# Tap pairs over all 128 rows in a key compression, and rotation tables of the index heads ahead of the others

## The chip, the core and the metric

The kernel runs on one core of one Trainium2 chip. The metric is device time in microseconds of one execution. In the profile, PE is TensorE's matmul, PEld its weight load, DVE is VectorE, ACT is ScalarE, POOL is GpSimd and SP is SyncE, which here issues nearly all DMAs.

## The reference, cut to what matters

Two decoder layers over 256 tokens of width 1024, float32. Each has a token mixer, a cross-attention into 256 memory tokens and a SwiGLU FFN. Layer 0's mixer holds a sparse attention whose index heads score every key (rotated index queries against rotated index keys, ReLU, a weighted sum over 8 heads), keep the top 64 keys of each query, and attend to them. Layer 1's mixer has among its branches a compressed one:

```
def nsa_compress(x, pos_emb, w1, w2):              # x (1, 256, 4 groups, 64)
    n_cmp = (S - 32) // 16 + 1                     # 15 blocks of 32 tokens, 16 apart
    blk = x[:, idx] + pos_emb[None, None, :, None, :]
    blk = ....reshape(B, n_cmp, G, 32 * 64)
    return jax.nn.silu(blk @ w1) @ w2              # w1 (2048, 64), w2 (64, 64)
```

It runs once for keys and once for values, with weights of their own. Rotation (`partial_rope`) multiplies pairs of elements by cosines and sines of position times frequency. The index heads use it without a gain; the other heads use it with their norm's gain, which the kernel folds into their tables.

## The kernel before, in words

**Order of the work.** The program is unrolled by Python coroutines. A planner (`Steps`, `Est`) keeps an estimated clock for each engine and issues, again and again, the operation that can start first; among those within 0.03 us on one engine the lower rank goes first, then the earlier, then the one spawned first. Every engine then runs its list strictly in that order. One helper (line 252) puts out all compute instructions, so nearly every row bears that line, and rows are told apart by their tiles. An instruction whose operand is late holds up all that stand behind it on its engine. An operation with two ways (`move`, `tt`) goes to the engine that the planner thinks sooner. For a DMA the planner only notes an assumed landing time.

**Weights.** A coroutine `pusher` (line 458 on) takes 256 rows by 512 columns of a weight matrix at a time from a `raw` tile (3 of them), makes a rounded part `hi` (ACT or DVE) and a remainder `lo` (DVE, one `TENSOR_TENSOR` into `whl`), and issues the load of the pair three further on, on SP's queue. Six `whl` pairs can stand ready. Every large product is three float32r matmuls (`mm3`) into PSUM banks that the profile calls `mm` and, in the FFN's second product, also `po`.

**The start.** `tables()` (line 550), rank 3, makes angles from positions on DVE, sine and cosine on ACT, then waits until the first norm has written both halves of row tile 0 (`has(("mix0", 0), 2)`), and then makes the gain rows, the index heads' tables `ia` and `ib`, the other heads' tables `ra` and `rb`, and the masks `cm`, `cmn`, `cmi`; at its end it sets the flag `tables`. `ev_small` takes the first product's result (index queries, index keys and one key head) out of PSUM, waits for `tables`, rotates the index queries (`rope`), transposes, and so releases `index()`, whose sums on DVE are followed by `top()`: eight rounds of finding and striking out eight maxima, on DVE. The attention over the chosen keys waits for that (`bias`). The other three products of this mixer go on meanwhile.

**The compression.** `load_cmp()` is started when layer 0's FFN has issued its first products. It loads `w1` into four tiles, 64 rows of keys' weights above 64 rows of values' weights, `w2`, and the position rows. At the mixer's start `prep()` transposes the position rows into a fifth group of the tile `kvT`, and `ev_kc` writes there, row tile by row tile, the transposed keys (rows 0 to 63) and values (rows 64 to 127). `compress()` then goes over the 32 taps. Each tap has two matmuls, one for keys, one for values, each over 64 rows into 64 output rows, with 75 moving columns (5 groups of 15 blocks, 16 elements apart):

```
yield T.matmul(hps[64 * i:64 * i + 64, :NB], w1[tt // 8][0][64 * i:64 * i + 64, tt % 8, :],
         kvT[64 * i:64 * i + 64, :, tt:tt + 16 * (NCMP - 1) + 1:16],
         start=(tt == 0), stop=(tt == 31), tile_position=(64 * i, 64 * i))
```

The fifth group's column is the share of the position rows, copied to `pb` and used as the bias of the SiLU. After every 8 taps the coroutine lets at least one `mm3` of another product go in between. A float32 matmul stands in the trace as two pairs of a weight load and a matmul, so 64 matmuls are 128 records of each kind.

Of the kernel before, what the change touches and what calls it, by code (L numbers as in the profile page):

```python
# [8 lines left out]
F32 = mybir.dt.float32  # L9
F32R = mybir.dt.float32r  # L10
# [5 lines left out]
P = 128  # L16
# [72 lines left out]
class Steps:  # L89
# [7 lines left out]
    def spawn(self, g, rank=2):  # L97
        self.n += 1
        self.new.append([rank, self.n, g, None])
# [253 lines left out]
def trunk(ctx: ExitStack, tc: tile.TileContext, I, out):  # L353
# [196 lines left out]
    def tables():  # L550
# [21 lines left out]
        yield from ready(AF.Exp)  # L572
        yield has(("mix0", 0), 2)
# [17 lines left out]
        gv = growt.rearrange("p j (a b) -> p j a b", a=2)  # L591
        for h in range(2):
            yield V.tensor_copy(ia[:, :, h, :], cos[:, :, ::2])
            yield V.tensor_copy(ib[:, :, h, :], (sin if h else nsin)[:, :, ::2])
        for t in range(NT):
# [115 lines left out]
    def root(key, t):  # L711

        yield lambda: (key, t) in vr
        return vr[key, t]
# [124 lines left out]
    def mixer0():  # L839
# [11 lines left out]
        def ev_small(ps, free, t):  # L851
# [88 lines left out]
        def ev_q(j, key):  # L940
            def ev(ps, free, t):
                q, qf = yield from T2.get([P, 8, HD])
                yield move(q.rearrange("p h d -> p (h d)"), ps)
                yield from inv_rms(ps, 8, HD, (yield from root("mix0", t))[0], 1.0, HD, rq[j, t], free)
                yield from rope(q, 8, ra[:, t, 2 * j], rb[:, t, 2 * j], HALF)
# [12 lines left out]
        def ev_k(ps, free, t):  # L958
            q, qf = yield from T2.get([P, 8, HD])
            yield S.activation(q.rearrange("p h d -> p (h d)"), ps, AF.Copy)  # L960
            rk = tiny(8, "rk8")
            yield from inv_rms(ps, 8, HD, (yield from root("mix0", t))[0], 1.0 / HD, 1.0, rk, free)
            yield from rope(q, 8, ra[:, t, 3], rb[:, t, 3], HALF)
            dd, df = yield from T4.get([P, 8, 2, HD])
# [78 lines left out]

    def load_cmp():
        w2 = hp.tile([P, P], F32, name="w2")
        pos = hp.tile([32, P], F32, name="posemb")
        yield PO.memset(w2, 0.0)
        w1 = []
        for j in range(4):
            w = yield from SL.get([P, 8, HD])  # L1050
            w1.append(w)
            for i, s in enumerate("kv"):
                nc.sync.dma_start(w[0][64 * i:64 * i + 64],
                                    I[f"nsa_cmp_w1_{s}"][0, 512 * j:512 * j + 512].rearrange("(t d) h -> d t h", d=HD))
        for i, s in enumerate("kv"):
            nc.sync.dma_start(w2[64 * i:64 * i + 64, 64 * i:64 * i + 64], I[f"nsa_cmp_w2_{s}"][0])
            nc.sync.dma_start(pos[:, 64 * i:64 * i + 64], I[f"nsa_cmp_pos_{s}"][0])
        w1s.update(w1=w1, w2=w2, pos=pos)
        done("cmpw")

    def mixer1():
# [3 lines left out]
        gt = [hp.tile([P, G * HG, 3], F32, name=f"gt{t}") for t in range(NT)]  # L1065
        kvT = hp.tile([P, G + 1, SEQ], F32, name="kvT", tag="kvT")
# [4 lines left out]
        def prep():  # L1071
            yield has("cmpw")
            yield PO.memset(kvT[:, G, 32:], 0.0)
            ps, f = yield from TP.get([P, 512])
            yield T.transpose(ps[:, :32], w1s["pos"], ident[:32, :32])
            yield V.tensor_copy(kvT[:, G, :32], ps[:, :32])
            f()
            done("kvT")

        def ev_kc(ps, free, t):  # L1080
            c, cf = yield from T2.get([P, G, 2, HD])
            yield S.activation(c, ps.rearrange("p (b g d) -> p g b d", b=2, g=G), AF.Copy, scale=(yield from root("mix1", t))[1])
            free()
            tps, f = yield from TP.get([P, 512])
            for g in range(G):
                yield T.transpose(tps[:, g * P:(g + 1) * P], c[:, g].rearrange("p a d -> p (a d)"), ident)
            yield S.activation(kvT[:, :G, t * P:(t + 1) * P], tps.rearrange("p (a b) -> p a b", a=G), AF.Copy)
            f()
            cf()
            done("kvT")  # L1090

        def compress():
            yield has("kvT", 3)
            NB = (G + 1) * NCMP
            N = G * NCMP
            w1 = w1s["w1"]
            hps, hf = yield from PV.get([P, 512])
            for tt in range(32):
                if tt % TAPS == 0 and tt:
                    yield has("mm", flags["mm"] + 1)  # L1100
                for i in range(2):
                    yield T.matmul(hps[64 * i:64 * i + 64, :NB], w1[tt // 8][0][64 * i:64 * i + 64, tt % 8, :],
                             kvT[64 * i:64 * i + 64, :, tt:tt + 16 * (NCMP - 1) + 1:16],
                             start=(tt == 0), stop=(tt == 31), tile_position=(64 * i, 64 * i))
            for w in w1:
                w[1]()
            pb = tiny(1, "pb")
            yield V.tensor_copy(pb, hps[:, N:N + 1])
            hs = tp.tile([P, N], F32, name="hs")
            yield S.activation(hs, hps[:, :N], AF.Silu, bias=pb)  # L1110
            hf()
# [200 lines left out]
        h = [hsel(t) for t in range(NT)]  # L1312
        spawn(prep())
        spawn(compress())
# [48 lines left out]
    def mem_k(L):  # L1363
        kT = [hp.tile([P, MH, SEQ], F32R, name=f"mkT{e}") for e in range(2)]
        mkv[L, "k"] = kT
# [273 lines left out]
```

## Time and profile before

| | |
|---|---|
| three timed runs | 784.57, 785.92, 786.65 us (median 785.92) |
| the profiled execution | 785.81 us, of which the span is 784.0 |
| PE busy | 757.2 us (97%) |
| DVE, ACT, POOL busy | 531.3, 435.7, 122.7 us (68%, 56%, 16%) |
| mean granted TensorE clock | 0.995 |

The span runs from the first to the last instruction, and 1.8 us of the execution's time lie around it. A busy share is a mean over stages: the start, the two mixers and the FFNs differ. In the list of records a matmul's duration holds its way through the array too, and neighbours overlap, so the pace of a run of matmuls is read from the distance between starts.

### The profile page before, as it was taken

Reading aid. Unit: us, or ns where it says so; the run is one execution under the profiler, and the core shown is the slowest. Engines: PE = TensorE matmul, PEld = TensorE weight load, DVE = VectorE, ACT = ScalarE, POOL = GpSimd, SP = SyncE. Lnnn points to the kernel's source line nnn. Section 1 sums busy time; section 2 is a strip of 40 time slices with the busy share of each in tenths; the row PEclk is TensorE's granted clock in tenths of the full one; section 3 lists DMA queues with packets and bytes.
Section 4 is the critical chain, followed back from the end, with each engine's and each line's share of the span. In section 5 each row is a group of like instructions: output and inputs, shape, how many; then the busy total and the mean of one; then the engine's idle time right before and its main releaser. Section 6 shows DMA issues by size and latency. Waiting matters only on the chain.

```text
span 784.0 us, 11770 instructions
## 1 busy us (share of the span) xinstructions
PE 757.2 (97%) x4227; PEld 629.6 (80%) x4227; DVE 531.3 (68%) x1111; ACT 435.7 (56%) x819; POOL 122.7 (16%) x169
## 2 busy tenths in 40 slices
PE   6898899999999999999999999999999999999998
PEld 5777687798888888878788787887888888889886
DVE  6899998778655545555717889978767546546542
ACT  5677786566545444344525889846656444444440
POOL 1554430210000000000106365301200000000000
PEclk9999899999999999999999999999999999999999
DMA  6735424435465554777524723034435566546761
GB/s 213 207 101 162 147 96 159 164 108 168 156 210 179 164 185 122 203 243 229 172 58 129 219 77 110 14 122 163 160 115 167 162 201 188 165 130 214 221 184 54
DMA packets 70635, 122.32 MB, mean 156 GB/s; under 512 B 8549, under 2 KB 15793, under 8 KB 70577
## 3 DMA queue, kind: packets, MB, share of 16 engines
q1 hardware_dynamic: 70544, 121.58, 49.7%
q8 instruction: 33, 0.54, 0.3%
q14 instruction: 26, 0.20, 0.1%
q0 software_dynamic: 32, 0.00, 0.0%
HBM read 120.51 MB, written 1.05 MB: 155 GB/s over the span
## 4 chain that ended last, share of the span: by engine, by line
PE 73%; DVE 10%; DMA 6%; ACT 4%; POOL 3%; issue 3%; SPq 1%; ACTq 0%; POOLq 0%; DVEq 0%
PE mm L252 56%; PE po L252 9%; PE tp L252 6%; DVE whl L252 3%; DMA raw<-in_ffn_w_out 3%; PE sp L252 3%; DVE place L252 3%; ACT whl L252 2%; ACT place L252 2%; DMA raw<-in_nsa_w_in 2%; POOL rope L252 1%; DMA raw<-in_ab_w_in 1%; POOL place L252 1%; DVE hss L252 1%; DMA raw<-in_nsa_w_out 1%
## 5 line engine op out<-in xcount | busy, mean ns | idle before, releaser
L252 PE MATMUL mm<-whl,h 128*128 128x512 f32 (+3 forms) x1776 | 400.4, 379 | 3.6 <-DVE whl L252 3.2
L252 DVE TENSOR_TENSOR whl<-raw,whl 128x1024 fp32r<-128x1024 f32 (+3 forms) x232 | 272.2, 1180 | 135.6 <-ACT whl L252 133.4
L252 PEld LDWEIGHTS mm<-whl,h 128*128 128x128 f32 x1776 | 310.5, 189 | 60.8 <-DVE whl L252 4.1
L252 ACT ACTIVATE whl<-raw 128x1024 fp32r<-128x1024 f32 (+3 forms) x216 | 218.3, 1012 | 193.0 <-PE mm L252 75.4
L252 PE MATMUL mm<-whl,place 128*128 128x512 f32 (+1 forms) x840 | 195.3, 376 | 0.9 <-DVE x L252 0.8
L252 PEld LDWEIGHTS mm<-whl,place 128*128 128x128 f32 x840 | 143.4, 190 | 28.2 <-DVE x L252 1.6
L252 PE MATMUL po<-whl,place 128*128 128x512 f32 x264 | 68.1, 395 | 0.0
L252 ACT ACTIVATE place<-tp 128x512 f32<-128x512 f32 (+4 forms) x115 | 54.7, 500 | 20.9 <-PE tp L252 20.4
L252 PEld LDWEIGHTS po<-whl,place 128*128 128x128 f32 x264 | 49.4, 188 | 11.4
L252 PE MATMUL tp<-ident,place 128*128 128x128 f32 (+1 forms) x340 | 53.1, 276 | 4.7 <-POOL place L252 2.3
L252 PEld LDWEIGHTS tp<-ident,place 128*128 128x128 f32 (+1 forms) x340 | 40.1, 140 | 13.9 <-issue 3.5
L252 ACT ACTIVATE place<-place,mx 128x128 f32<-128x128 f32 (+1 forms) x96 | 42.9, 453 | 7.7 <-DVE mx L252 6.6
L252 POOL TENSOR_TENSOR place<-place,rc 128x512 f32<-128x512 f32 (+2 forms) x33 | 29.7, 900 | 41.2 <-DVE rc L252 29.0
L252 POOL TENSOR_TENSOR rh<-vh,mhalf 128x1 f32<-128x1 f32 x12 | 9.9, 826 | 148.5 <-DVE vh L252 132.2
L252 ACT ACTIVATE h<-place 128x512 fp32r<-128x512 f32 x23 | 14.4, 628 | 33.0 <-DVE place L252 33.0
L252 DVE TENSOR_TENSOR x<-mm,x 128x512 f32<-128x512 f32 x36 | 24.5, 684 | 10.3 <-PE mm L252 10.2
L252 DVE CUSTOM_DVE_ANT_0 place<-sp,cm,rq 128x128 f32<-128x128 f32 (+1 forms) x80 | 30.3, 407 | 1.3 <-PE sp L252 1.2
L252 ACT ACTIVATE place<-mm 128x512 f32<-128x512 f32 (+2 forms) x45 | 23.0, 553 | 14.3 <-PE mm L252 14.3
L252 ACT ACTIVATE place<-mm,rh 128x512 f32<-128x512 f32 (+1 forms) x26 | 17.0, 654 | 22.4 <-PE mm L252 22.4
L252 DVE SCALAR_TENSOR_TENSOR place<-mm,rh,place 128x512 f32<-128x512 f32 (+1 forms) x24 | 16.9, 704 | 18.1 <-PE mm L252 18.1
L252 POOL TENSOR_TENSOR h<-place,h 128x512 fp32r<-128x512 f32 x1 | 1.3, 1294 | 175.9 <-ACT h L252 175.9
L252 PE MATMUL sp<-place,place 128*128 128x256 f32 x160 | 27.1, 300 | 0.0
(202 smaller groups left out, 620.4 us busy)
## 6 DMA issues: line engine op xcount, KB each, us to landing
raw<-in_ffn_w_in SPq DMA_DIRECT2D x80, 512.0 KB, 4.3
raw<-in_ffn_w_out SPq DMA_DIRECT2D x44, 512.0 KB, 4.3
raw<-in_ab_w_in SPq DMA_DIRECT2D x16, 512.0 KB, 4.1
raw<-in_mem_w_kv SPq DMA_DIRECT2D x16, 512.0 KB, 3.9
raw<-in_nsa_w_in SPq DMA_DIRECT2D x16, 512.0 KB, 4.1
raw<-in_ab_w_out SPq DMA_DIRECT2D x8, 512.0 KB, 3.8
raw<-in_mem_w_q SPq DMA_DIRECT2D x8, 512.0 KB, 4.0
raw<-in_mem_w_o SPq DMA_DIRECT2D x8, 512.0 KB, 4.1
```

The costliest lines, as they stand in the source:

```text
L252: return f(*a, **{q: v() if q in ("start", "stop") and callable(v) else v for q, v in k.items()})
```

## The change

`tables()` gets rank 2; right after the cosine it makes `ia` and `ib`, sets a new flag `angles`, and leaves the rest to a new coroutine `gains()` of rank 3. `ev_small` waits for `angles` before it rotates the index heads, and for `tables` only before it rotates the key head; the other three rotations of this mixer get a wait for `tables`.

In the compression, taps `j` and `j + 16` form a pair. There are now two tiles `kvT[i]` in place of one, with the elements in the order tap, group, block. `ev_kc` writes keys into rows 0 to 63 of the first and values into rows 64 to 127 of the second, and when both row tiles are there, two DMAs on ACT's queue copy each to the other 64 rows, one element on, which is the next block of the same tap. A matmul then goes over 128 rows (both taps of the pair) into 64 output rows with 60 moving columns (4 groups, each of 15 neighbouring blocks); keys and values take the two column halves of the array. `load_cmp` loads `w1` in the matching order, the position rows with two DMAs more, and itself works out the position rows' share, `pb`, by products with `w1` and sums on DVE or POOL and a matmul of one column. `prep()` is gone. The new tiles take the tag of the memory keys `mkT`.

```
@@ tables
+        for h in range(2):
+            yield V.tensor_copy(ia[:, :, h, :], cos[:, :, ::2])
+            yield V.tensor_copy(ib[:, :, h, :], (sin if h else nsin)[:, :, ::2])
+        done("angles")
+        spawn(gains(sin, nsin, cos), 3)
+
+    def gains(sin, nsin, cos):
+        yield has(("mix0", 0), 2)
...
@@ ev_small
-            yield has("tables")
+            yield has("angles")
             yield from rope(c[:, 128:384].rearrange("p (h d) -> p h d", h=IH), IH, ia[:, t], ib[:, t], IHALF)
...
+            yield has("tables")
             yield from rope(k, 1, ra[:, t, 1], rb[:, t, 1], HALF)
...
@@ load_cmp
+        for i, s in enumerate("kv"):
+            for j in range(2):
+                w = yield from SL.get([P, 8, HD])
+                w1.append(w)
+                for b in range(2):
+                    d0 = HD * (16 * (b ^ i) + 8 * j)
+                    nc.sync.dma_start(w[0][64 * b:64 * b + 64], I[f"nsa_cmp_w1_{s}"][0, d0:d0 + 512].rearrange("(t d) h -> d t h", d=HD))
+                est.note(w[0], est.wr, clk["PE"] + 8.0, "D")
...
+        est.note(pos, est.wr, clk["PE"] + 8.0, "D")
+        ps, f = yield from TP.get([P, 512])
+        yield T.transpose(ps[:, :32], pos, ident[:32, :32])
+        yield V.tensor_copy(pT.rearrange("p a b -> p (a b)"), ps[:, :32])
+        f()
+        for i in range(2):
+            u = []
+            for j in range(2):
+                u.append((yield from SL.get([P, 8, HD])))
+                yield tt(u[j][0], w1[2 * i + j][0], pT[:, i, 8 * j:8 * j + 8, None].to_broadcast([P, 8, HD]), OP.mult)
+            yield tt(u[0][0], u[0][0], u[1][0], OP.add)
+            u[1][1]()
+            yield V.tensor_reduce(red[:, i], u[0][0].rearrange("p t h -> p h t"), axis=AX.X, op=OP.add)
+            u[0][1]()
+        ps, f = yield from TP.get([P, 512])
+        yield T.matmul(ps[:, :1], red.rearrange("p a b -> p (a b)"), one, start=True, stop=True)
+        yield V.tensor_copy(pb, ps[:, :1])
...
@@ ev_kc
-            yield S.activation(kvT[:, :G, t * P:(t + 1) * P], tps.rearrange("p (a b) -> p a b", a=G), AF.Copy)
+            for i in range(2):
+                r = slice(64 * i, 64 * i + 64)
+                yield S.activation(kvT[i][r, :, :, 8 * t:8 * t + 8].rearrange("p j g n -> p g n j"),
+                                   tps[r].rearrange("p (g n j) -> p g n j", g=G, n=8), AF.Copy)
...
+                for i in range(2):
+                    a, b = (kvT[i][64 * e:64 * e + 64].rearrange("p j g n -> p (j g n)") for e in (i, 1 - i))
+                    nc.scalar.dma_start(b[:, :-1], a[:, 1:])
+                    est.note(b, est.wr, clk["S"] + 3.0, "D")
...
@@ compress
-            for tt in range(32):
-                if tt % TAPS == 0 and tt:
+            for j in range(16):
+                if j % TAPS == 0 and j:
                     yield has("mm", flags["mm"] + 1)
...
+                yield together([T.matmul(hps[64 * i:64 * i + 64, :N], w1s["w1"][2 * i + j // 8][0][:, j % 8, :],
+                                         kvT[i][:, j, :, :NCMP], start=(j == 0), stop=(j == 15), tile_position=(0, 64 * i))
+                                for i in range(2)])
...
-    spawn(tables(), 3)
+    spawn(tables(), 2)
```

## Rows read from the trace of the kernel before

**Rows 1.** The page's first part: busy time and share of each engine.

```profile
PE 757.2 (97%) x4227; PEld 629.6 (80%) x4227; DVE 531.3 (68%) x1111; ACT 435.7 (56%) x819; POOL 122.7 (16%) x169
```

**Rows 2.** Stretches: us; busy PE, PEld, DVE, ACT, POOL; PEclk, DMA share, GB/s.

```profile
8.70:20.00 11.30, 10.62 (x43) 9.20 (x44) 11.09 (x27) 8.04 (x17) 1.08 (x2) 1.00 0.73 216
20.00:42.00 22.00, 18.98 (x85) 14.85 (x84) 17.89 (x60) 14.37 (x24) 12.33 (x22) 1.00 0.74 214
42.00:60.00 18.00, 17.80 (x104) 14.59 (x105) 16.85 (x40) 13.64 (x26) 9.89 (x18) 1.00 0.25 69
60.00:72.00 12.00, 11.02 (x55) 8.73 (x53) 12.00 (x33) 7.99 (x16) 5.88 (x8) 1.00 0.40 126
72.00:79.00 7.00, 5.66 (x30) 4.42 (x29) 7.00 (x29) 6.10 (x12) 1.82 (x1) 1.00 0.81 258
79.00:87.30 8.30, 7.24 (x47) 5.96 (x45) 8.27 (x46) 6.15 (x25) 3.36 (x5) 1.00 0.19 69
87.30:94.20 6.90, 5.13 (x30) 3.92 (x29) 6.87 (x16) 5.50 (x11) 3.41 (x3) 0.65 0.51 174
331.00:376.00 45.00, 43.99 (x189) 34.96 (x187) 22.66 (x19) 19.10 (x18) 0.00 (x0) 1.00 0.73 232
...
89.40:96.30 6.90, 6.43 (x25) 5.10 (x26) 6.82 (x20) 5.88 (x15) 2.20 (x2) 0.51 0.72 237
```

**Rows 3.** The chain of waits, 300 to 460 us: start, length, what.

```profile
324.37 1.39 PE po L252 x6
325.76 0.30 SPq L1053
...
400.31 2.18 PE po L252 x32
402.50 0.43 PE mm L252
...
409.11 2.19 PE po L252 x32
```

**Rows 4.** Instructions in order of time on PE, 495.9 to 500 us: start, length.

```profile
496.10 0.97 PE L252 MATMUL sp<-kbd,place 128*128 128x30 f32 x8
496.91 0.72 PE L252 MATMUL sp<-place,place 128*128 128x256 f32 x4
...
498.27 1.04 PE L252 MATMUL po<-place,place 120*64 120x128 f32 x16
499.24 0.98 PE L252 MATMUL sp<-place,place 128*128 128x256 f32 x6
```

**Rows 5.** Instructions in order of time, 0 to 42 us: the index heads' way.

```profile
18.75 0.51 ACT L252 ACTIVATE place<-mm 128x424 f32<-128x424 f32 x1
...
24.70 0.21 ACT L252 ACTIVATE cos<-ang 128x16 f32<-128x16 f32 x1
...
28.44 0.15 DVE L252 COPY ia<-cos 128x8 f32<-128x8 f32 x1
...
28.66 0.16 DVE L252 COPY ib<-sin 128x8 f32<-128x8 f32 x1
...
31.48 0.32 POOL L252 TENSOR_TENSOR rope<-place,ia 128x64 f32<-128x64 f32 x1
```

**Rows 6.** SP's issues in order of time, 310 to 335 us: first and last of twelve.

```profile
321.23 0.72 SPq L1053 DMA_DIRECT2D place<-in_nsa_cmp_w_k  x1
...
330.00 0.58 SPq L1057 DMA_DIRECT2D posemb<-in_nsa_cmp_pos_v  x1
```

**Rows 7.** Instructions in order of time, 346 to 394 us: end of layer 0's FFN.

```profile
374.17 1.23 DVE L252 TENSOR_TENSOR whl<-raw,whl 128x1024 fp32r<-128x1024 f32 x1 [1.26 <-ACT whl L252]
375.31 0.68 DVE L252 TENSOR_TENSOR x<-mm,x 128x512 f32<-128x512 f32 x1
376.05 0.66 PE L252 MATMUL tp<-ident,x 128*128 128x128 f32 x4 [0.93 <-DVE x L252]
```

**Rows 8.** DMA issues by group: count, KB each, us from issue to landing.

```profile
out_x<-x SPq DMA_DIRECT2D x4, 256.0 KB, 2.0
```

More of the change, by code (lines that the diff above doesn't have):

```diff
@@ L591, in tables @@
         gv = growt.rearrange("p j (a b) -> p j a b", a=2)
-        for h in range(2):
-            yield V.tensor_copy(ia[:, :, h, :], cos[:, :, ::2])
-            yield V.tensor_copy(ib[:, :, h, :], (sin if h else nsin)[:, :, ::2])
         for t in range(NT):
@@ L944, in ev @@
                 yield from inv_rms(ps, 8, HD, (yield from root("mix0", t))[0], 1.0, HD, rq[j, t], free)
+                yield has("tables")
                 yield from rope(q, 8, ra[:, t, 2 * j], rb[:, t, 2 * j], HALF)
@@ L962, in ev_k @@
             yield from inv_rms(ps, 8, HD, (yield from root("mix0", t))[0], 1.0 / HD, 1.0, rk, free)
+            yield has("tables")
             yield from rope(q, 8, ra[:, t, 3], rb[:, t, 3], HALF)
@@ L1046, in load_cmp @@
         pos = hp.tile([32, P], F32, name="posemb")
+        pT = hp.tile([P, 2, 16], F32, name="posT")
+        red = hp.tile([P, 2, HD], F32, name="posw")
+        pb = hp.tile([P, 1], F32, name="posb")
         yield PO.memset(w2, 0.0)
         w1 = []
[L1049 to L1054, printed above, removed]
+        for i, s in enumerate("kv"):
[6 more added lines that the diff above has]
+                est.note(w[0], est.wr, clk["PE"] + 8.0, "D")
@@ L1055, in load_cmp @@
         for i, s in enumerate("kv"):
             nc.sync.dma_start(w2[64 * i:64 * i + 64, 64 * i:64 * i + 64], I[f"nsa_cmp_w2_{s}"][0])
-            nc.sync.dma_start(pos[:, 64 * i:64 * i + 64], I[f"nsa_cmp_pos_{s}"][0])
-        w1s.update(w1=w1, w2=w2, pos=pos)
+            for b in range(2):
+                nc.sync.dma_start(pos[16 * i:16 * i + 16, 64 * b:64 * b + 64], I[f"nsa_cmp_pos_{s}"][0, 16 * (b ^ i):16 * (b ^ i) + 16])
+        est.note(pos, est.wr, clk["PE"] + 8.0, "D")
+        ps, f = yield from TP.get([P, 512])
@@ L1065, in mixer1 @@
         gt = [hp.tile([P, G * HG, 3], F32, name=f"gt{t}") for t in range(NT)]
-        kvT = hp.tile([P, G + 1, SEQ], F32, name="kvT", tag="kvT")
+        kvT = [hp.tile([P, 16, G, 16], F32, name=f"kvT{i}", tag=f"mkT{i}") for i in range(2)]
         kbd = hp.tile([P, G, 2, NCMP], F32, name="kbd")
@@ L1069, in mixer1 @@
         vbig = {}
[L1071 to L1078, printed above, removed]
         def ev_kc(ps, free, t):
@@ L1090, in ev_kc @@
             done("kvT")
+            if has("kvT", NT)():
+                for i in range(2):
+                    a, b = (kvT[i][64 * e:64 * e + 64].rearrange("p j g n -> p (j g n)") for e in (i, 1 - i))
+                    nc.scalar.dma_start(b[:, :-1], a[:, 1:])
+                    est.note(b, est.wr, clk["S"] + 3.0, "D")
+                done("kvT")
         def compress():
             yield has("kvT", 3)
-            NB = (G + 1) * NCMP
             N = G * NCMP
+            yield has("cmpw")
             w1 = w1s["w1"]
             hps, hf = yield from PV.get([P, 512])
-            for tt in range(32):
-                if tt % TAPS == 0 and tt:
+            for j in range(16):
+                if j % TAPS == 0 and j:
                     yield has("mm", flags["mm"] + 1)
[L1101 to L1104, printed above, removed]
+                yield together([T.matmul(hps[64 * i:64 * i + 64, :N], w1s["w1"][2 * i + j // 8][0][:, j % 8, :],
+                                         kvT[i][:, j, :, :NCMP], start=(j == 0), stop=(j == 15), tile_position=(0, 64 * i))
+                                for i in range(2)])
             for w in w1:
                 w[1]()
-            pb = tiny(1, "pb")
-            yield V.tensor_copy(pb, hps[:, N:N + 1])
             hs = tp.tile([P, N], F32, name="hs")
-            yield S.activation(hs, hps[:, :N], AF.Silu, bias=pb)
+            yield S.activation(hs, hps[:, :N], AF.Silu, bias=w1s["pb"])
             hf()
@@ L1312, in mixer1 @@
         h = [hsel(t) for t in range(NT)]
-        spawn(prep())
         spawn(compress())
@@ L1363, in mem_k @@
     def mem_k(L):
-        kT = [hp.tile([P, MH, SEQ], F32R, name=f"mkT{e}") for e in range(2)]
+        kT = [hp.tile([P, MH, SEQ], F32R, name=f"mkT{e}", tag=f"mkT{e}") for e in range(2)]
         mkv[L, "k"] = kT
```

3 lines of the change are left out of this document (2 added, 1 removed).

## The prediction, as it was put on record

> **What bounds the kernel now.** I read the page's busy shares first: PE is busy for 757.2 of 784.0 us, so the reader is to see a kernel in which a change pays only if it takes work off PE or closes one of the few holes in PE's time [rows 1]. Where the holes lie stands in the table by stretches: from 20 to 42 us PE lacks 22.00 - 18.98 = 3.02 us, from 42 to 60 us 0.20, and from 60 to 94.2 us 0.98, 1.34, 1.06 and 1.77 us [rows 2]. In those last four stretches DVE is full (12.00 of 12.00, 7.00 of 7.00, 8.27 of 8.30, 6.87 of 6.90 us): there DVE is the bound and PE waits for it. From 89.40 to 96.30 us the mean granted clock is 0.51, which is nearly all at 1.2 GHz, after PE's thin stretches from 72 us on; the 6.43 us that PE was busy in it would have taken about half at 2.4 GHz, so 3.2 us went there [rows 2]. The chain of waits then shows which of the rest counts: around 400 us it runs on PE alone, through four blocks of the compression's matmuls, 2.18 to 2.20 us each [rows 3].
>
> **The compression.** Its four blocks hold 32 records each, and four times 2.19 us is 8.76 us, 68.4 ns a record [rows 3]. After the change there are 16 taps by two halves, 32 matmuls, 64 records, so the count halves. The new shape (128 rows into 64, 60 columns) isn't in the trace. Nearest from above is the shape of 120 rows into 64 with 128 columns, two column halves in turn: 16 records between 498.27 and 499.24 us, 60.6 ns each. Nearest from below is a record that is almost only weight load, 128 weight columns and 30 moving ones: 8 records between 496.10 and 496.91 us, 101 ns, so an estimated 50.6 ns for 64 weight columns [rows 4]. I take 56 ns, the middle: 64 x 56 = 3.6 us, with 3.2 and 3.9 as the bounds, and 4.4 us if the record costs what the old one did. The saving is 8.76 - 3.6 = 5.16 us. Each change of shape costs too: the single product matmul between two blocks takes 0.43 us on the chain, where six of 512 columns in the FFN take 1.39 us, 0.23 each, so the edges of a block cost 0.20 us; two blocks go, 0.4 us [rows 3]. New on PE is the matmul of one column for `pb`, two records, 0.2 us by the 101 ns row; the position rows' transpose is only moved. Together: 5.16 + 0.4 - 0.2 = **5.36 us less on PE**, between 4.2 (the old price a record and no edge saved) and 5.8 (the low bound).
>
> This stays to the end, because nothing else is late there: everything behind the compression, weight pairs included, is released by PE's own progress.
>
> **What must land first.** The compression now waits for two copies from SBUF to SBUF of about 256 KB each, behind the evacuation of the second row tile. The nearest row is the store of the same size, 2.0 us to landing [rows 8]; with two issues at about 0.6 us each (0.58 for the last of SP's twelve [rows 6]) the second lands about 3.2 us after the evacuation, and the planner has noted 3.0. PE has the next product to do meanwhile. The wait is 0 to 1 us; I charge 0.2. The evacuation itself becomes four ACT instructions in place of two, beside PE's products. Behind the waiting matmul all of PE is queued, and ACT's SiLU with it.
>
> **The loading.** `load_cmp` issues 14 DMAs on SP in place of 12, about 1.2 us more by 0.6 each [rows 6], and the `raw` loads queue behind. That shifts the weight pairs by 1.2 us. PE doesn't starve, but at 375 us the residual sum on DVE stands behind a `whl` subtraction that ended just then, and PE lost 0.93 us waiting for it [rows 7]. If that subtraction comes 1.2 us later the hole grows by up to 1.2 us; if the planner puts the sum first it doesn't grow. I charge a third, 0.4 us. The new sums (four products and two additions of 128x512, by the residual row's 0.68 us, and two reductions of the same size: some 5.5 us if all go to DVE) lie in 331 to 376 us, where DVE is busy 22.66 of 45.00 us [rows 2, 7]; I cost them at nothing. Without that cover each could hold a `whl` subtraction up by 0.68 us. PE's transpose of the position rows comes forward from the mixer's start to right behind these DMAs; that is a rival below.
>
> **The tables.** The first product's result for row tile 0 leaves PSUM at 18.75 us; the cosine is made at 24.70, `ia` at 28.44, and the first rotation of the index queries starts only at 31.48 us, because it waits for all tables [rows 5]. Afterwards it needs the cosine and four copies. With rank 2 and the first place among equals the 16 small DVE steps of the angles run as soon as they can, so I expect the rotation at 20 to 25 us, some 7 us earlier, and with it the index sums, the top-64 rounds and the attention. What that gives is bounded by DVE, full from 60 us on: only what DVE does earlier, in its holes from 20 to 60 us (22.00 - 17.89 + 18.00 - 16.85 = 5.26 us), ends earlier [rows 2]. I take 3.0 us of it as filled, somewhat over half, since part of the holes are waits for ACT's rounding. Against it, the 16 small steps move to 8 to 14 us, where DVE is busy 11.09 of 11.30 us and feeds the first products: four such copies take 0.07 us apart each (28.44 to 28.66 for three steps), so 16 cost up to 1.2 us, all of which I charge [rows 2, 5]. Net **1.8 us**. The ends: 1.2 us lost if no hole is filled; 8.4 us gained if all of PE's holes from 60 to 94.2 us (5.15 us) and the slow clock (3.2 us) go.
>
> **Sum**, against the profiled execution's own 785.81 us (0.1 us under the median of 785.92): 785.81 - 5.36 - 1.8 + 0.2 + 0.4 = **779.2 us**.
>
> **Rivals.**
> 1. The tables bring nothing: DVE is full from 60 us and merely does the same work in another order. For it speaks the full DVE, against it the 5.26 us of holes before. Then 785.81 - 5.36 + 0.6 = 781.1 us, and 782.3 with the 1.2 us lost.
> 2. The tables bring much: the attention begins while products are still left, PE never thins out at 72 to 94 us and the clock stays at 2.4 GHz. For it speaks that PE's holes and the slow clock lie just where the attention over the chosen keys is alone; against it that DVE paces that attention too. Then as low as 785.81 - 5.36 - 8.4 + 0.6 = 772.7 us.
> 3. Weight load and matmul of the new shape don't overlap. From rows: 50.6 ns of load and 60/75 of 68.4 = 54.7 ns of columns, 105 ns a record, 6.7 us for 64, so 785.81 - (8.76 - 6.7 + 0.4 - 0.2) - 1.8 + 0.6 = 782.4 us. Against it speaks the 60.6 ns row: 128 columns in the same two halves leave no room for a load in series [rows 4]. The Trainium skill ("TensorE: Matmul & The Clock Gate", Part 3 on packing small matmuls) has the rule that makes this rival: a weight load overlaps running matmuls only if the row group differs. The old pair differs in its rows, the new one has all 128 in common, so by that rule the change would give up an overlap; the trace speaks against the rule for this shape.
> 4. **Slower**: PE waits in `load_cmp`. The transpose of the position rows stands in PE's order for when the planner thinks them landed (8 us after the last weight tile was placed), but they are the last of 14 DMAs on SP, issued only as slots come free. Before, the last of 12 was issued at 330.0 to 330.58 us, and nothing on PE needed it soon. If the slots come free at once by the planner, at about 321 us of PE's time, the transpose stands at 329 us, the rows land at about 333.8 (330.58 + 1.2 + 2.0), and PE stands still 4.6 us and then runs at 1.2 GHz for a while, as after the holes before 89 us (3.2 us): 785.81 - 5.36 - 1.8 + 0.6 + 7.8 = 787.1 us, and over 788.2 with rival 1 or with a `raw` load held up too. From 7 us of standing still it decides. Against it: the chain passes from PE to SP's weight tiles at 325.76 us, so one of them waited for a slot until then, which puts the planner's 8 us at 333.8 too [rows 3, 6].
> 5. The change doesn't do what it says: the planner, with all its times moved, loses elsewhere in the mixers what the compression gives. Then 784 to 788 us.
>
> **How the numbers follow.** Forecast, 777 to 781 us: 0.40. Rival 1: 0.22. Rival 2, under 777: 0.20. Rival 3: 0.04. Rival 4: 0.08, half of it past 788.2. Rival 5: 0.06. About 0.3%, 2.4 us, is what a measurement of this kernel can tell from no change: faster is under 783.5, slower over 788.2. The first four cases, save a little, are faster, 0.84; rivals 4 and 5 leave 0.11 for the same and 0.05 for slower. The range 772.0 to 784.0 leaves out the rest of rivals 4 and 5 and an extreme of rival 2.
>
> **What would show it.** Right: 64 records of the new shape in two blocks of 1.6 to 2.0 us; no pause on PE ahead of the first; the first rotation of the index queries before 26 us; PE's holes from 60 to 94 us smaller by 2 to 3 us. Wrong: records at 100 ns; PE idle for a DMA near 330 or 400 us; the stretch of half clock still there, or a new one; the first product later by more than 1.2 us. A DVE hole from 20 to 60 us as large as before would refute the tables' step.

## The result, and the profile after

The changed kernel took **790.36 us** (median of four runs, 789.50 to 791.72) beside 785.25 for the kernel before (four runs, 784.27 to 786.65): a ratio of 1.0071, interval 1.0056 to 1.0085. It is slower by 5.1 us; the prediction was 779.2 us, in a range of 772 to 784. The profiled execution took 790.44 us, with a span of 788.7 and a mean granted clock of 0.990 (before: 785.81, 784.0, 0.995).

The page's first part, as in [rows 1]:

```profile
PE 752.9 (95%) x4165; PEld 626.5 (79%) x4165; DVE 537.3 (68%) x1123; ACT 437.2 (55%) x817; POOL 123.9 (16%) x168
```

PE has 4.3 us less work and the span is 4.7 us longer: PE stands still for 9 us more. Where it does shows when both traces are asked at what time the same weight product begins (the n-th weight load of a `whl` tile; 2880 in each trace; us):

| the product of | before | after | after - before |
|---|---|---|---|
| behind layer 0's first mixer product | 22.3 | 23.5 | +1.1 |
| behind the next of its products | 34.7 | 38.4 | +3.7 |
| that mixer's output product, first | 93.2 | 97.3 | +4.1 |
| layer 0's FFN, ahead of its second product | 313.7 | 315.4 | +1.7 |
| that second product, 72 of 264 done | 336.5 | 345.6 | +9.2 |
| that second product, 216 of 264 done | 370.3 | 382.3 | +12.0 |
| mixer 1, ahead of the compression | 396.3 | 406.7 | +10.4 |
| mixer 1, just behind it | 419.3 | 423.1 | +3.8 |
| mixer 1's first output product | 489.0 | 496.6 | +7.7 |
| the last of all | 779.6 | 784.2 | +4.7 |

Four things are to be seen: a loss at the start, of which 1.7 us are left at the FFN, a loss of 10.3 us in the FFN's second product, a gain of 6.6 us at the compression, and a few us that come and go in mixer 1.

**The loss in the FFN.** PE's instructions in order of time, 319 to 360 us (start, length, what, and in brackets the idle time before and what ended it):

```profile
335.68 0.28 PE L252 MATMUL tp<-ident,posemb 32*128 32x32 f32 x1 [5.16 <-DMA posemb<-in_nsa_cmp_pos_v]
335.90 2.50 PE L252 MATMUL mm<-whl,place 128*128 128x512 f32 x5
338.20 2.29 PE L252 MATMUL po<-whl,place 128*128 128x512 f32 x6
340.33 1.54 PE L252 MATMUL mm<-whl,place 128*128 128x512 f32 x6
...
347.27 1.09 PE L252 MATMUL po<-whl,place 128*128 128x512 f32 x4
351.15 0.35 PE L252 MATMUL tp<-one,posw 128*128 128x1 f32 x2 [2.79 <-DVE posw L252]
```

PE stood still twice for `load_cmp`: 5.16 us for the position rows' DMA, and 2.79 us for their sum `posw`. Between the two, the eleven products from 335.90 to 340.33 us took 4.43 us; at the pace of the chain before (six in 1.39 us, [rows 3]) they take 2.55, so 1.9 us went to the clock. With the two new matmuls themselves (335.68 to 335.90 and 351.15 to 351.36 us, 0.43) that makes 5.16 + 2.79 + 1.9 + 0.4 = 10.3 us, the whole loss. Busy time by stretch, with the columns of [rows 2]:

```profile
330.50:335.70 5.20, 0.04 (x2) 0.05 (x1) 1.11 (x1) 0.00 (x0) 0.00 (x0) 0.74 0.39 89
335.70:340.10 4.40, 4.40 (x12) 3.46 (x13) 0.88 (x1) 1.47 (x2) 0.00 (x0) 0.53 0.97 350
340.10:348.40 8.30, 8.26 (x36) 6.38 (x34) 8.27 (x11) 3.59 (x4) 1.49 (x1) 1.00 0.58 161
348.40:351.20 2.80, 0.05 (x1) 0.08 (x1) 2.78 (x4) 1.30 (x2) 0.00 (x0) 1.00 0.68 232
331.00:376.00 45.00, 37.53 (x154) 30.12 (x155) 23.96 (x25) 15.91 (x15) 1.49 (x1) 0.92 0.65 198
```

The last row is what I read before, and again DVE is busy barely half of it, 23.96 of 45.00 us. But from 340.10 to 351.20 us it was busy 11.05 of 11.10 us. The granted clock behind the first pause is 0.53, nearly all at 1.2 GHz. SP's issues (to be held against [rows 6]) and DVE's instructions of the same time:

```profile
323.25 2.99 SPq L1067 DMA_DIRECT2D place<-in_nsa_cmp_w_k  x4
...
333.25 1.04 SPq L1072 DMA_DIRECT2D posemb<-in_nsa_cmp_pos_v  x2
334.39 1.41 SPq L444 DMA_DIRECT2D raw<-in_ffn_w_out  x3
```

```profile
339.22 1.22 DVE L252 TENSOR_TENSOR whl<-raw,whl 128x1024 fp32r<-128x1024 f32 x1 [7.61 <-ACT whl L252]
340.37 0.18 DVE L252 COPY posT<-tp 128x32 f32<-128x32 f32 x1
340.58 2.14 DVE L252 TENSOR_TENSOR place<-place,posT 128x512 f32<-128x512 f32 x2
...
348.84 1.21 DVE L252 TENSOR_TENSOR whl<-raw,whl 128x1024 fp32r<-128x1024 f32 x1
349.98 1.02 DVE L252 TENSOR_REDUCE posw<-place 128x64 f32<-128x512 f32 x1
```

SP is kept by `load_cmp` from 323.25 to 334.39 us and loads no FFN weights meanwhile, so DVE waits 7.61 us for weights to subtract. Then the sums and the overdue subtractions meet on DVE, and PE's one-column matmul waits for the last of the sums. The kernel before had the same late weights, without a loss. Its DVE, of the same time:

```profile
335.93 3.86 DVE L252 TENSOR_TENSOR whl<-raw,whl 128x1024 fp32r<-128x1024 f32 x3 [6.78 <-ACT whl L252]
```

It waited 6.78 us and then had three subtractions to make up, but PE went on from the pairs in stock (43.99 of 45.00 us busy, [rows 2]). What is new is an instruction in PE's stream that needs a result from behind such a burst.

**The gain.** The compression on PE, in place of the four blocks of 2.19 us in [rows 3]:

```profile
413.84 0.33 PE L252 MATMUL po<-kvT,place 128*64 128x60 f32 x2
414.86 1.11 PE L252 MATMUL po<-kvT,place 128*64 128x60 f32 x30 [0.70 <-DMA kvT<-kvT]
415.90 0.74 PE L252 MATMUL mm<-whl,h 128*128 128x512 f32 x2
416.57 1.15 PE L252 MATMUL po<-kvT,place 128*64 128x60 f32 x32
```

Thirty records from 414.86 to 415.90 us are 34.7 ns each, about 34 in the second block: half of the old 68.4. After two records PE waits for the second copy, which the tile's list shows as landing 3.4 us after its issue.

**The start**, beside [rows 5]:

```profile
20.28 0.20 ACT L252 ACTIVATE cos<-ang 128x16 f32<-128x16 f32 x1
20.50 1.28 ACT L252 ACT_TABLE_LOAD   x1
21.01 0.16 DVE L252 COPY ia<-cos 128x8 f32<-128x8 f32 x1
22.52 0.50 ACT L252 ACTIVATE place<-mm 128x424 f32<-128x424 f32 x1
24.48 0.20 DVE L252 TENSOR_TENSOR rope<-place,ia 128x64 f32<-128x64 f32 x1
```

The cosine is 4.4 us earlier and the first rotation 7.0 us. But the first product leaves PSUM at 22.52 us, where it left at 18.75. Of these 3.8 us PE's part is small: the last of the product's 24 matmuls for row tile 0 begins at 18.52 us, before at 17.69, 0.8 us later. The rest is ACT's order: a weight rounding (18.70 us), parts of the next norm and, new in this place, the cosine with a table load of 1.28 us behind it stand ahead of the evacuation; before, those last two came at 24.70 and 24.93 us, after it.

### The profile page after: what moved, and what is told of

Its sections match the earlier page's. It is cut to its first block, busy times and chain, and to the rows that moved or that the text cites. A ratio compares the mean times of both kernels' runs of the same rounds, so it can differ in the third digit from the quotient of the medians.

```text
span 788.7 us, 11669 instructions
## 1 busy us (share of the span) xinstructions
PE 752.9 (95%) x4165; PEld 626.5 (79%) x4165; DVE 537.3 (68%) x1123; ACT 437.2 (55%) x817; POOL 123.9 (16%) x168
## 4 chain that ended last, share of the span: by engine, by line
PE 73%; DVE 13%; DMA 5%; ACT 3%; issue 2%; POOL 2%; SPq 1%; ACTq 0%; DVEq 0%; POOLq 0%
PE mm L252 56%; PE po L252 9%; PE tp L252 5%; DVE whl L252 4%; DVE place L252 4%; PE sp L252 2%; DMA raw<-in_ab_w_in 2%; ACT place L252 2%; ACT whl L252 1%; DMA raw<-in_ffn_w_out 1%; DVE hss L252 1%; POOL rope L252 1%; DVE rc L252 1%; DMA raw<-in_ffn_w_in 1%; DMA raw<-in_nsa_w_in 1%
## 5 line engine op out<-in xcount | busy, mean ns | idle before, releaser
L252 DVE TENSOR_TENSOR whl<-raw,whl 128x1024 fp32r<-128x1024 f32 (+3 forms) x232 | 268.8, 1165 | 137.5 <-ACT whl L252 135.7
L252 ACT ACTIVATE whl<-raw 128x1024 fp32r<-128x1024 f32 (+2 forms) x215 | 217.5, 1012 | 204.2 <-PE mm L252 72.9
L252 PEld LDWEIGHTS sp<-place,place 128*128 128x128 f32 x160 | 22.9, 196 | 3.7 <-DVE mx L252 1.0
```

What stands on the lines that cost most here:

```text
L252: return f(*a, **{q: v() if q in ("start", "stop") and callable(v) else v for q, v in k.items()})
```

## The experiments

Each was timed beside the kernel before on its own chip, whose median there was 784.9 to 785.6 us; the ratio (with its interval) is the measure.

### The two parts apart

**tables_only**: the kernel before with the tables' part of the change alone. **pairs_only**: the changed kernel with the tables as before.

> The kernel before with the tables' part of the change alone (rank 2, index tables first, the waits moved); the compression is the old one. Counting the weight products done on PE, the changed kernel was 2.1 us behind the kernel before at the end of layer 0's cross-attention, ahead of any change in the compression. Theory, the tables cost that by themselves: 785.3 + 1.7 to 2.2 = 787 to 787.5 us. Rival, the lag is only an effect of the planner seeing other work later (the programs of the two differ nowhere else before that point, so this should not be): 785.3 us. Rival, as I had predicted, a gain of about 1.8 us: 783.5 us.

Measured 786.85 us, ratio 1.0015 (0.9999 to 1.0031): no gain, and probably a small loss.

> The changed kernel with the tables' part undone; compression and loading as changed. Theory, the parts add: PE loses about 10.3 us at the position rows (5.2 us for their DMA, 2.8 us for the sum, 2.2 us at half clock), gets back about 1.6 us of it by the next mixer, wins 6.6 us in the compression: 785.3 + 8.7 - 6.6 + 0.9 = 788.3 us. Rival, the wait for the position rows comes from the lag that the tables put on PE, so it goes with them: 780 us or less.

Measured 791.81 us, 1.0087 (1.0073 to 1.0102). The pairs alone lose all that the change loses, with both waits in `load_cmp` (3.90 and 3.29 us). The tables' part is innocent of them.

### What PE waits for in `load_cmp`

**late_note** (changed kernel) and **pairs_late** (with the old tables): the planner takes the position rows for landed 8 us later.

```
-        est.note(pos, est.wr, clk["PE"] + 8.0, "D")
+        est.note(pos, est.wr, clk["PE"] + 16.0, "D")
```

> The changed kernel with one number changed: the planner is told that the position rows land 16 us, not 8, after it places them. Theory, PE's transpose then stands behind more products in PE's order, no wait for the DMA, no fall of the clock after it, and no wait for the sum: 790.4 - 8.7 = 781.7 us, and tables' lag left in. Rival 1, the wait for the sum stays (DVE is full there): 784.5 us. Rival 2, the weights are what is late (14 DMAs on SP ahead of the next weight loads), the products starve at the same place instead: 788 us or more.

Measured 791.97 us, 1.0090 (1.0074 to 1.0107).

> The compression by pairs with the later landing time of 16 us, and the old tables: both costs taken out. Theory: 785.3 - 6.6 + 0.9 = 779.6 us, within 1.5 us. Rival, the win in the compression is given back in the mixer's DVE-bound stretch: 783 us or more.

Measured 791.66 us, 1.0089 (1.0073 to 1.0105). The wait for the DMA is gone in both, and the time stays: the other wait has grown to 9.04 and 9.08 us. PE and then DVE of pairs_late, and its busy time by stretch:

```profile
354.84 0.56 PE L252 MATMUL tp<-one,posw 128*128 128x1 f32 x2 [9.08 <-DVE posw L252]
```

```profile
336.37 3.89 DVE L252 TENSOR_TENSOR whl<-raw,whl 128x1024 fp32r<-128x1024 f32 x3 [8.27 <-ACT whl L252]
...
346.15 0.18 DVE L252 COPY posT<-tp 128x32 f32<-128x32 f32 x1
...
353.68 1.01 DVE L252 TENSOR_REDUCE posw<-place 128x64 f32<-128x512 f32 x1
```

```profile
345.60:354.80 9.20, 0.16 (x1) 0.00 (x0) 9.10 (x12) 2.79 (x3) 1.49 (x1) 0.70 0.56 168
354.80:362.00 7.20, 7.16 (x23) 5.84 (x24) 2.75 (x4) 2.12 (x2) 0.00 (x0) 0.68 0.72 212
```

PE transposed the position rows at 336.63 us, but DVE copied the result only at 346.15, behind subtractions of weights that had come late. The planner had put them in this order with a full stock of weight pairs in mind, which the loading had used up; the trace doesn't show what the planner had in mind, but pairs_know below, which tells it of the loading, bears this out. So the missing operand was only the first of two prices: a PE instruction in the FFN's stream that depends on DVE work behind the weights.

**pairs_sum_later** (old tables) and **changed_sum_later** (the whole change): transpose, sums and column matmul wait for mixer 1.

```
         est.note(pos, est.wr, clk["PE"] + 8.0, "D")
+        yield has("mixer1")
@@ mixer1
+        done("mixer1")
         spawn(compress())
```

> Old tables, the compression by pairs, loads as changed, but the position rows' transpose, sums and column matmul are held back until layer 1's mixer starts. Theory (the column matmul stalls PE because its sums stand on DVE behind weight subtractions six pairs ahead of PE, and just after the loads that stock isn't there): no stall, the compression's win of about 7.0 us stays, less some 2 us that the DVE-bound mixer gives back: 785.6 - 5 = 780.6 us. Rival, the loads themselves or the pairs cost the time: 786 us or more. Rival, the sums only stall PE at their new place: 785 us or more.

Measured 782.83 us (780.52 to 786.89), 0.9969 (0.9951 to 0.9986): faster than before, and 1.2% better than pairs_only, of 1.0087.

> The changed kernel, tables included, with the sums held back until layer 1's mixer. Theory, the tables cost about 1.2 us by themselves and the rest is as in the kernel with old tables: 782 us. Rival, the tables gain once PE doesn't stall behind them: under 780 us.

Measured 785.48 us, 0.9994 (0.9980 to 1.0007): the whole change without the waits in `load_cmp` is level with the kernel before. Both runs lost something else: by the lags of the table the compression gains 3.0 and 3.3 us in them, where the changed kernel gained 6.6. The copies landed 5.0 to 5.6 us after their issue, and in pairs_sum_later PE stood still 1.99 us ahead of the first pair (the profile names no cause) and 0.56 us for a copy. So the two show that the waits in `load_cmp` go with the sums, and less than the whole of what the waits cost.

**pairs_know** (old tables): the sums stay, but the planner learns of the loading; each of the 14 DMAs moves its DMA clock on by 0.75 us, and the landings are noted from that clock.

```
+        def dma(o, i):
+            nc.sync.dma_start(o, i)
+            clk["D"] = max(clk["D"], est.now) + 0.75
...
-        est.note(pos, est.wr, clk["PE"] + 8.0, "D")
+        est.note(pos, est.wr, max(clk["D"], clk["PE"]) + 2.0, "D")
```

> Old tables, the compression by pairs, sums where the change put them; only the planner's clock of the DMAs is moved on by 0.75 us for each of load_cmp's 14 DMAs, and the landing times are taken from it. Theory (what is wrong is that the planner doesn't know that the weight loads stand behind those DMAs): the transpose and the column matmul now stand on PE where DVE, at the pace of the late weights, has done the sums; the wait for them falls from 9.1 us to under 2 us: 785.6 - 7 + 2 + up to 2 = 781 to 783 us. Rival, DVE's own load in that stretch is what makes the sum late, whatever the planner knows: the wait stays above 5 us and the time above 786 us.

Measured 784.10 us, 0.9983 (0.9972 to 0.9993). No wait for the rows or `posw` is left, with the sums where the change put them; the time is above the 781 to 783 us that were expected. What remains there are two holes of 1.86 and 2.08 us, for weights and the residual sum.

### The pace of the compression

**two_banks**: the kernel before, keys' and values' halves in two PSUM banks.

```
-                    yield T.matmul(hps[64 * i:64 * i + 64, :NB], ...
+                    yield T.matmul(two[i][64 * i:64 * i + 64, :NB], ...
```

> The kernel before, with the keys' and the values' sums of the old compression in two PSUM banks instead of one; 32 taps and 64 rows as before. It asks why a record of the old shape took 68.4 ns and one of the new 34. Theory A, the two halves of the old shape stand in different rows and can't write one bank at the same time: with two banks they overlap, 128 records in some 4.4 to 5 us instead of 8.76, and the kernel is about 4 us faster, 781.5 us. Theory B, halves that differ in rows don't run side by side anyway: 68 ns a record as before, 785.6 us.

Measured 784.68 us, 0.9989 (0.9979 to 0.9999). Its trace decides better than its time:

```profile
398.51 0.32 PE L252 MATMUL po<-kvT,place 64*64 64x75 f32 x1
398.52 0.32 PE L252 MATMUL tp<-kvT,place 64*64 64x75 f32 x1
398.66 0.30 PE L252 MATMUL po<-kvT,place 64*64 64x75 f32 x1
...
400.69 0.50 PE L252 MATMUL mm<-whl,h 128*128 128x512 f32 x1
```

A block of 32 records goes from 398.51 to 400.69 us, 2.18 us as before. The shared bank wasn't what held the old pair. The Trainium skill ("TensorEngine Tiling (Array Packing)", Gotcha 1) says that different row tiles can't access one bank at a time; no price of that shows in the two traces. Both halves begin within 0.01 us of each other in the shared bank too, and each begins its next after 0.13 us. So the small gain in time isn't the bank's; its cause is open.

### What a shorter compression is worth

**half_taps**: the kernel before, with taps 0 to 15 only.

```
-            for tt in range(32):
+            for tt in range(16):
```

> The kernel before, whose compression goes over taps 0 to 15 only; the other 16 taps are left out of the sum, and nothing else is changed. What is disputed is how much of PE time taken out of the compression reaches the end. 64 records of 68.4 ns and two edges of 0.2 us are gone, 4.8 us. Theory A (my prediction: all behind the compression is released by PE's own progress): 785.3 - 4.8 = 780.5 us, the lag of 4.8 us standing unchanged to the last weight product. Theory B (mixer 1 gives part back, since from 470 us DVE is full and PE thins out, as in the kernel whose DMA clock knows the loads, where 6.8 us at the compression were 2.9 at the end): about 783 us, with PE's holes and half clock between 470 and 490 us larger than before.

Measured 783.61 us, 0.9970 (0.9959 to 0.9981): of the estimated 4.8 us taken out, 2.0 reached the end (1.5 to 3.2 by the ratio's interval). In its trace, by the same weight products as in the table above, the lead is 0.2 us ahead of the compression, 5.5 just behind it, 4.9 at the last product of the queries (440.6 us, before 445.5), gone at the first output product (489.9 us, before 489.0), and 2.4 at the end. One wait on PE, and busy time by stretch, of half_taps:

```profile
446.70 0.51 PE L252 MATMUL tp<-identr,t 128*128 128x128 f32 x4 [2.95 <-DVE t L252]
```

```profile
430.00:450.00 20.00, 17.05 (x87) 13.96 (x86) 15.00 (x30) 13.21 (x21) 4.92 (x4) 1.00 0.70 205
...
470.00:490.00 20.00, 17.96 (x185) 15.09 (x184) 19.47 (x87) 19.36 (x64) 12.47 (x15) 1.00 0.26 84
...
440.00:490.00 50.00, 44.30 (x372) 36.70 (x371) 45.18 (x182) 42.33 (x131) 26.74 (x33) 1.00 0.33 105
```

The same stretch of the kernel before, from its last queries to its first output product:

```profile
445.00:489.00 44.00, 41.16 (x347) 35.29 (x345) 39.88 (x158) 39.10 (x121) 24.83 (x33) 1.00 0.36 112
```

PE, being early, has 5.7 us of holes there in place of 2.8. From 470 to 490 us DVE and ACT are full (19.47 and 19.36 us of 20). But DVE had room from 430 to 450 us (15.00 of 20) and didn't use it, so it isn't DVE's sum of work alone. The edit also made the planner write another order for this stretch; the run doesn't tell a dependence from that order. But the loss is no accident of one order: from just behind the compression to the end PE loses 0.4 to 3.7 us on the kernel before in each of the twelve traces with a shorter compression (0.9 in the changed kernel, 3.1 here), and 0.0, 0.0 and 0.7 us in the three with the old one (two_banks, tables_rank3, tables_only).

**pairs_engine_copy** (on pairs_sum_later): in place of the two DMA copies, four more evacuations into the other 64 rows, by ACT or DVE. **pairs_all_three**: this, the held sums and the DMA clock together.

```
+                q = slice(64 - 64 * i, 128 - 64 * i)
+                yield move(kvT[i][q, :, :, 8 * t - t:8 * t + 7].rearrange("p j g n -> p g n j"),
+                           tps[r].rearrange("p (g n j) -> p g n j", g=G, n=8)[:, :, 1 - t:])
...
-                    nc.scalar.dma_start(b[:, :-1], a[:, 1:])
```

> The kernel with old tables and the sums held back to mixer 1, in which the two DMA copies are replaced by four more evacuations straight out of PSUM into the other 64 rows, by ACT or DVE. In its parent PE stood still 2.0 + 0.6 us for the copies, which landed 5.1 to 5.6 us after their issue, and then ran the second block at half clock (1.97 for 1.15 us). Theory A (the copies' landing is a price of its own): 3 us less than the parent's 782.8, 780 us, no pause ahead of the compression. Theory B (mixer 1 gives back whatever the compression's end gains): 782 to 783 us. The four evacuations of about 1.1 us on ACT or DVE are beside PE in both.

Measured 785.76 us, 1.0004 (0.9992 to 1.0017).

> The kernel with old tables, the sums held back to mixer 1, the planner's DMA clock moved on by the loads, and copies by ACT and DVE in place of DMAs: all that the runs so far name as a price of the pairs is away. Theory A: what my prediction gave the pairs without the tables, 785.3 - 5.4 = 780 us or a little less. Theory B (mixer 1 gives back half): 782 to 783 us.

Measured 785.86 us, 1.0002 (0.9991 to 1.0013). Both theories missed: it is worse than the copies. PE of pairs_engine_copy, whose waits have only changed their name:

```profile
400.67 0.66 PE L252 MATMUL tp<-ident,place 128*128 128x128 f32 x4 [1.28 <-ACT place L252]
405.67 1.76 PE L252 MATMUL po<-kvT,place 128*64 128x60 f32 x30 [1.75 <-ACT kvT L252]
```

### The tables' rank

**tables_rank3**: tables_only, but with `tables()` at rank 3 as before. The index heads still have their own flag.

> The kernel before with the tables split and the flag for the index heads, but the rank left at 3. Theory A (what the tables' part costs comes from its 16 small DVE steps that go ahead of the first products): 785.0 to 785.6 us, and the first weight products end no later than before. Theory B (it comes from the index sums on a DVE that is full, wherever they start): 786.5 to 787 us, as with rank 2. Theory C (my prediction's step, an earlier index path gains once nothing is pushed back): 783 us.

Measured 783.75 us, 0.9979 (0.9968 to 0.9990). The split alone is 1.9 us faster than before, and rank 2 turns that into nothing or a loss. The index heads' way and two stretches of tables_rank3:

```profile
19.49 0.51 ACT L252 ACTIVATE place<-mm 128x424 f32<-128x424 f32 x1
...
25.25 0.21 ACT L252 ACTIVATE cos<-ang 128x16 f32<-128x16 f32 x1
...
27.30 0.33 POOL L252 TENSOR_TENSOR rope<-place,ia 128x64 f32<-128x64 f32 x1 [0.26 <-DVE ib L252]
```

```profile
87.30:94.20 6.90, 6.03 (x49) 4.65 (x48) 6.90 (x24) 6.85 (x24) 2.69 (x3) 1.00 0.80 237
94.20:105.00 10.80, 10.73 (x95) 8.84 (x94) 10.77 (x44) 8.51 (x27) 6.10 (x7) 1.00 0.43 132
```

The cosine comes no earlier than before, and still the rotation is 4.2 us earlier, since it no longer waits for the other tables. The first product is 0.7 us late instead of 3.8 in the changed kernel, the last search for maxima begins at 81.2 us (88.7 before, 83.5 in tables_only), and the granted clock stays at 1.00, all at 2.4 GHz, where it was 0.65 before [rows 2]. What differs there is that products are left beside the attention: the last weight load of the mixer's four products begins at 91.9 us, against 85.1 before and 85.5 in the changed kernel. So the gain goes with this order, as far as one trace of each shows; why the planner finds it at rank 3 and not at rank 2 is open.

**changed_rank3** and **changed_rank3_later**: the changed kernel, and changed_sum_later, with `tables()` at rank 3.

```
-    spawn(tables(), 2)
+    spawn(tables(), 3)
```

> The changed kernel with tables() at rank 3, and nothing else. If the rank costs the same here as in the kernel before (786.9 at rank 2, 783.8 at rank 3): 790.4 - 3.1 = 787.3 us, still slower than before by the pause of the sums. Rival: with the sums' pause of 10 us behind it, what the tables gain or lose at the start is swallowed: 789.5 to 791 us.

Measured 788.07 us, 1.0035 (1.0022 to 1.0048): of the changed kernel's 5.1 us over the kernel before, 3.2 are left.

> The changed kernel with its position sums held back to mixer 1 and tables() at rank 3 as before: both causes that the runs name are away, and the rest of the change is whole. If they are separate (sums held back: 2.4 us under the kernel before; tables at rank 3: 1.9 us under it), 785.4 - 2.4 - 1.9 = 781.1 us. Rival: the two gains meet in mixer 1, which gives back what comes early, as with half the taps (4.8 us taken out, 2.0 left): 782.5 to 783.5 us.

Measured 782.75 us (778.55 to 785.67), 0.9967 (0.9948 to 0.9987). This version of the whole change beats both kernels, but it isn't faster than pairs_sum_later. The two gains don't add. In the profiled execution, the slowest of its twelve, PE leads the kernel before by 2.6 us up to the FFN's second product, is 3.3 us behind ahead of the compression, after a hole of 3.34 us at 377.8 us for the residual sum (0.93 in [rows 7]), and 1.8 ahead behind it.

## Why the prediction was wrong

**The sums cost nothing** (cover: DVE busy 22.66 of 45.00 us) is the step that failed most. The two waits of `load_cmp` cost 10.3 us where I had charged 0.4 for the whole loading. In this trace 2.79 us of it stand against the sums, but with the first wait away theirs is 9.08 us and the time is the same (pairs_late). The mean that I read was right, and DVE is half idle on the mean after the change too. It said nothing of the order: the sums stand on DVE between subtractions that wait for weights, and the matmul behind them stands in PE's stream. I asked what each of the sums would delay, and not what waits for the sums.

**Rival 4, the pause for the position rows** (787.1 us, chance 0.08) was the right mechanism and nearly the right size: 4.6 us of standing still (4.8 by its own 329 and 333.8) and 3.2 of slow clock said, 5.16 and 1.9 measured. I held against it that the planner's 8 us would end at 333.8 us. The transpose stood at 330.5, and the rows landed at 335.7; SP had begun its first weight tile only at 323.25 us, where it was 321.23 before. What the rival missed is the second wait, and pairs_late shows that it fills whatever the first one leaves. Holding the sums back removed both: 1.0087 to 0.9969 with the old tables, 1.0071 to 0.9994 in the changed kernel.

**The compression**, -5.36 us, was mis-sized, on the safe side. At 34 ns a record, under my low bound of 50.6, the stretch from the product ahead to the product behind it fell from 396.3 to 419.3 us (23.0) to 406.7 to 423.1 (16.4), 6.6 us less, copies' wait included. The two rows from which I had bounded the price were unlike it: one had 128 weight columns, the other 128 moving ones. **Rival 3** is refuted: it priced a record at 105 ns, and one takes 34. As the trace lists them, a record's weight load lasts 138 ns (median) while records begin 34 ns apart, so loads and matmuls overlap. The Trainium skill ("TensorE: Matmul & The Clock Gate", Part 3) says that a weight load overlaps running matmuls only where the row group differs; the trace disagrees for these two column halves of the same 128 rows.

**The copies' wait**, 0.2 us, was 0.7; they landed 3.4 us after their issue, not 2.0, and 5.3 to 5.6 us in pairs_sum_later.

**The loading's 0.4 us**, for a larger hole at the residual sum, had the wrong sign. SP's next FFN load was issued 3.7 us later than before (334.39 us, before 330.68), 2.0 us of it because `load_cmp` began later and 1.7, where 1.2 were said, because it took longer; but with PE later by 12 us the sum found DVE free: PE's hole of 0.93 us [rows 7] is gone, and 1.2 us of the lag with it.

**"This stays to the end"** failed too. Half the taps show it without any other change to the work: 2.0 of 4.8 us arrive. In the changed kernel's trace 5.7 of the 6.6 us arrive, so this step isn't what made it slower. My reason, that PE's own progress releases all that follows, holds for the products but not for mixer 1's attention. Rival 5 had this, at 0.06. Which dependence holds the attention isn't settled: DVE and ACT are full from 470 us on, but have room 20 us earlier.

**The tables**, -1.8 us, had the right idea and missed by the rank. The rotation came at 24.48 us as forecast (20 to 25), and DVE's holes from 20 to 60 us did shrink, from 5.26 to 2.79 us (20.07 and 17.14 busy, below). PE's first product came 0.8 us later, within the 1.2 charged for the 16 small steps. What I had not charged is ACT: with the cosine and the table load ahead of it, the evacuation that the rotation needs came 3.8 us later. PE's holes from 60 to 94.2 us, forecast to be 2 to 3 us smaller, went from 5.15 to 4.85 us, and the slow clock, a sign of being wrong, is still there, only later: 0.69 from 94.20 to 105.00 us. The mixer's output product began 4.1 us later than before, in spite of the earlier rotation. Without the rank the split gives 1.9 us and loses the slow clock, as rival 2 had it, at much less than its 8.4 us. Rows of after that answer to [rows 2]:

```profile
20.00:42.00 22.00, 20.31 (x99) 15.74 (x98) 20.07 (x66) 17.35 (x35) 10.83 (x20) 1.00 0.66 191
42.00:60.00 18.00, 16.32 (x86) 13.09 (x85) 17.14 (x42) 12.20 (x21) 8.73 (x14) 1.00 0.51 143
60.00:72.00 12.00, 12.00 (x64) 9.99 (x62) 11.68 (x40) 7.56 (x15) 7.04 (x11) 1.00 0.36 115
72.00:79.00 7.00, 5.33 (x28) 3.91 (x26) 7.00 (x19) 5.60 (x12) 6.02 (x8) 1.00 0.51 152
79.00:87.30 8.30, 8.21 (x53) 7.01 (x52) 8.19 (x42) 4.75 (x20) 2.90 (x5) 1.00 0.24 93
87.30:94.20 6.90, 3.81 (x32) 2.65 (x32) 6.90 (x26) 6.90 (x23) 1.26 (x2) 0.99 0.34 116
94.20:105.00 10.80, 10.10 (x60) 8.76 (x61) 9.03 (x36) 7.61 (x25) 3.19 (x4) 0.69 0.38 114
```

**The account**, by the table of lags: +1.7 up to the FFN's second product, +10.3 in it, -1.6 from there to the compression (1.2 of it at the residual sum), -6.6 at the compression, +0.9 from there to the end: +4.7 us. By the runs, the pairs alone lose 6.2 us and the tables at rank 2 alone 1.3, against 5.1 for both; parts don't add to better than 2 or 3 us here, since every edit makes the planner write a new order.

## What to carry to other kernels

Work that is moved into another engine's slack has to be followed to its reader: a helper engine that is half idle on the mean can still be late when its operands come in a burst, and an instruction that waits for it in the critical engine's in-order stream stops everything behind it. Put such a reader where its operands are surely there, or keep it out of that stream until they are. And before a saving on the busiest engine is booked to the end, take the same time out by itself (here, half the taps): it shows what the stages behind give back.

## What the runs showed of the hardware

- Float32 matmuls of 128 rows into 64 columns with 60 moving columns, in the array's two column halves in turn, go at 34 ns a record; the diagonal pair of 64 rows into 64 columns with 75 moving ones went at 68 ns, in one PSUM bank or in two.
- Copies of 256 KB within SBUF landed 3.4 us after their issue in the changed kernel and 5.3 to 5.6 us in pairs_sum_later, at nearly the same DMA share about them (0.63 from 410 to 415 us, 0.64 from 401.6 to 408.2; 170 and 179 GB/s); why they differ is open. An ACT evacuation of 64 rows by 512 elements that permutes them takes 1.08 to 1.11 us, where the old one, of 128 by 512, took 0.60.
- After a pause of 5.16 us on PE the granted clock was 0.53 over the next 4.40 us; after one of 9.08 us it was 0.68 over 7.20 us; after the 2.79 us pause at 351 us the products went on at 1.40 us for six, at full clock. But after pauses of 2.88 us in changed_rank3 and 3.29 us in pairs_only it was 0.50 over 6.00 us and 0.78 over 7.60 us, so the length of a pause by itself doesn't tell whether the clock falls.
